# Two transformer blocks on one core: norm scales folded into the transposing product, the norm between the blocks rewritten, three up pieces in the last group

## The chip, the core and the metric

The kernel runs on one core of one Trainium2 chip. The metric is the device time of one execution in microseconds (us), lower is better. The engines are named as the profile names them: PE is TensorE (matmuls; PEld is its weight load), DVE is VectorE, ACT is ScalarE, POOL is GpSimd, SP is SyncE, whose queue issues the weight loads.

## The reference

Two blocks follow one another on 256 tokens of width 1024, in float32. The first has gated linear attention and sparse attention, a cross attention to 256 memory rows and a product-key expert layer ("peer"); the second has a gated recurrence (hgrn), a long convolution (hyena) and another peer layer. Each part starts with an RMS norm over the row. Two of these norms meet between the blocks: the first block's final norm, and the second block's first norm of its result.

```python
def rms_norm(x, g):
    y = x * lax.rsqrt(jnp.mean(x * x, axis=-1, keepdims=True) + EPS)
    return y * g

def first_block(x, mem, ...):
    hn = rms_norm(h, norm_mix)
    h = h + concat([gla_mixer(...), nsa_mixer(...)]) @ w_out
    h = h + cross_attn(rms_norm(h, norm_xattn), rms_norm(mem, norm_mem), ...)
    h = h + peer_ffn(rms_norm(h, norm_ffn), ...)     # 16384 experts, gelu(x @ down.T) * gate @ up
    return rms_norm(h, norm_final)

def second_block(x, ...):
    h = x + hybrid_mixer(rmsnorm(x, norm_mix_g), ...)
    h = h + peer_ffn_2(rmsnorm(h, norm_ffn_g), ...)
    return rmsnorm(h, norm_final_g)
```

The peer layers choose 16 experts per head for each token. The kernel computes them densely: all 16384 down products, a gate that is zero where an expert was not chosen, and all 16384 up products.

## The kernel before

**Products in three terms.** Each float32 operand is split into a high part (rounded to the fp32r type) and a low part (the rest), and `mm3` (L344 to L346) adds three products: high by high, low by high, high by low. A weight tile of 128x1024 is read by `load` (L250) on SP's queue into `wf`, of which there are four buffers, so a load starts when the tile four before it has been used up. `stream` makes the two parts: `wh` by an ACT cast (L318), `wl` by a DVE subtraction (L325, some of them on POOL), three buffers each. `dfth`, `dftl`, `idfth` and `idftl` (L491, L492) are the same two parts of the Fourier matrices that the second block needs; they are made while the first block ends. Behind most loads SP also issues a write of zeros of 512 KB (`gates<-zero`, L265), by which the second peer layer's gate table is cleared.

**A norm ahead of a product.** `norm_cols` turns 256 rows into columns for PE. `norm_rows` squares and sums each row in two halves (L391 on ACT, one on DVE), adds the halves (L410), forms mean plus epsilon (L381), raises it to the power -1/2 on POOL (L382), and scales the rows into a tile `xn`: three halves on DVE (L403), one on ACT (L404). This runs for the tokens' first half (t = 0) and second half (t = 1). `to_cols` then turns each 128x128 piece of `xn` on PE (L420: eight pieces for t = 0, eight for t = 1, into four PSUM banks of two pieces each), and `split` multiplies by the gain and makes the two parts `xch` (ACT, L430) and `xcl` (DVE, L433). There are five such sites: the start, the memory rows (about 95 to 110 us), the cross attention (213 to 229), and ahead of the two peer layers (`peer_in`, 316 to 328 and 1514 to 1523).

**Between the blocks.** `between` (L1416 to L1442, 1124 to 1141 us) does both norms at once. For each half of the tokens and each half of the columns it adds the peer sum from PSUM to the residual (L1425, `hres`), multiplies by the final gain (L1427, `hmid`), and takes the squares of both (`ssh` of `hres`, `ssy` of `hmid`). From the two sums follow two factors by small DVE operations (L1431 to L1434) and two POOL powers (L1437): one scales `hmid` to the second block's input, the other `hmid` to the first block's result (L1442, a whole row of 1024 each). `xn` is made by L1438 (DVE) and L1439 (ACT), and turned and split as above. The first tiles of the second block (`w2t`) are streamed behind it.

**The end of a peer layer.** `up` (L1082 to L1099) takes the 128 up tiles one by one: 12 matmuls of 128x512 for each, three on each of the four accumulating banks (two halves of the tokens by two halves of the columns). `ah` (ACT, L1078) and `al` (DVE, L1080) are the parts of the gated activations. The last two tiles are taken together, bank by bank, so that the first banks are complete earlier than the last. Behind the second peer layer `finish` (L1444 to L1461) adds, norms and writes the result.

**What sets the order.** Each engine works through its queue in order. A scheduler puts the instructions in an order by priorities; `after` adds an order between two instructions on one engine, and in `stream` and `norm_rows` it holds the first weight parts behind a norm (`self.ahead`).

## Time and profile before

| | us |
|---|---|
| timed, median of 3 runs | 2361.08 (2359.76 to 2364.35) |
| profiled execution, its own time | 2355.96 |
| span in the profile | 2354.2 |
| PE busy | 2307.6 |
| PE not busy | 46.6 |
| DVE, ACT, POOL busy | 1675.5, 1240.8, 471.6 |

The profiled execution is 5.12 us (0.2%) under the median of the timed runs. Busy times are taken over the whole span, so an engine that is nearly always busy hides the places where it waits; these places are found in the timeline, where each group of instructions has its start, its length and, in brackets, how long its engine was idle before it and what ended the wait. "PEclk" is the clock that TensorE was granted, as a share of 2.4 GHz: 0.50 is 1.2 GHz. A matmul's own length overlaps that of the next, so the distance between two starts is what one costs.

### The profile page before, as it was taken

To read this page: it belongs to the slowest core of one execution; us is meant where nothing else is said; L and a number is where in the kernel's file an instruction comes from. 1 tells how busy PE (TensorE), PEld (TensorE's weight loads), DVE (VectorE), ACT (ScalarE), POOL (GpSimd) and SP (SyncE) were. 2 spreads that over 40 slices of the span, in tenths; PEclk is the share of its full clock that TensorE was granted. 3 is DMA by queue.
4 is the path that set the end of the run, shared out by engine and by line. 5 is a ranking of instruction groups with operands and counts; after the bars stand their busy time and mean duration, and the time that the engine had idled before them with its cause. 6 is when DMAs were issued, how large, how long until landed. Compare 5 with 4: busy or idle time off the path is not lost.

```text
span 2354.2 us, 40890 instructions
## 1 busy us (share of the span) xinstructions
PE 2307.6 (98%) x15390; PEld 2100.5 (89%) x15390; DVE 1675.5 (71%) x3300; ACT 1240.8 (53%) x2368; POOL 471.6 (20%) x324
## 2 busy tenths in 40 slices
PE   8999999999999999999899999999999999999998
PEld 6976889999999888888899999899999999888886
DVE  6677559896677666666778886679886676666665
ACT  6555445456666444544654434445456665444444
POOL 0002000678760000000100000200787720000000
PEclk9999999999999999999999999999999999999999
DMA  7433565676555666666754444556675555666664
GB/s 236 137 119 98 161 224 170 175 185 161 149 148 155 221 201 201 197 201 194 249 173 130 150 153 144 181 175 183 164 187 152 149 148 194 198 203 199 203 202 134
DMA packets 149767, 412.26 MB, mean 175 GB/s; under 512 B 35980, under 2 KB 51521, under 8 KB 148417
## 3 DMA queue, kind: packets, MB, share of 16 engines
q1 hardware_dynamic: 129088, 409.57, 55.1%
q0 software_dynamic: 20480, 0.08, 2.4%
q8 instruction: 121, 1.98, 0.3%
q14 instruction: 78, 0.63, 0.1%
HBM read 394.83 MB, written 14.22 MB: 174 GB/s over the span
## 4 chain that ended last, share of the span: by engine, by line
PE 90%; DVE 7%; issue 1%; ACT 1%; POOL 1%; DMA 0%; POOLq 0%; SPq 0%; ACTq 0%
PE lin L346 16%; PE lin L344 16%; PE lin L345 16%; PE bank L346 11%; PE bank L344 11%; PE bank L345 10%; PE bank L1044 4%; DVE wl L325 2%; PE bank L1314 1%; PE bank L420 1%; PE bank L713 0%; ACT wh L318 0%; PE bank L832 0%; DVE cand L964 0%; POOL rstd L382 0%
## 5 line engine op out<-in xcount | busy, mean ns | idle before, releaser
L325 DVE TENSOR_TENSOR wl<-wf,wh 128x1024 fp32r<-128x1024 f32 (+1 forms) x698 | 853.3, 1224 | 301.7 <-ACT wh L318 296.8
L318 ACT CAST wh<-wf 128x1024 fp32r<-128x1024 f32 x704 | 734.8, 1045 | 610.2 <-PE lin L345 445.3
L344 PE MATMUL lin<-xch,wh 128*128 128x256 f32 x2912 | 836.6, 288 | 1.1 <-ACT wh L318 1.1
L346 PE MATMUL lin<-xch,wl 128*128 128x256 f32 x2912 | 827.5, 284 | 2.7 <-DVE wl L325 1.9
L345 PE MATMUL lin<-xcl,wh 128*128 128x256 f32 x2912 | 826.0, 284 | 0.0
L346 PEld LDWEIGHTS lin<-xch,wl 128*128 128x128 f32 x2912 | 559.3, 192 | 4.8 <-DVE wl L325 3.2
L344 PEld LDWEIGHTS lin<-xch,wh 128*128 128x128 f32 x2912 | 560.5, 193 | 3.0 <-ACT wh L318 1.4
L345 PEld LDWEIGHTS lin<-xcl,wh 128*128 128x128 f32 x2912 | 559.9, 192 | 0.0
L287 POOL DMA_INDIRECT gates<-gn,at x256 | 411.6, 1608 | 329.1 <-DVE gn L999 114.4
L346 PE MATMUL bank<-wh,al 128*128 128x512 f32 x1024 | 404.2, 395 | 0.0
L344 PE MATMUL bank<-wh,ah 128*128 128x512 f32 x1024 | 404.2, 395 | 0.0
L345 PE MATMUL bank<-wl,ah 128*128 128x512 f32 x1024 | 404.2, 395 | 0.0
L345 PEld LDWEIGHTS bank<-wl,ah 128*128 128x128 f32 x1024 | 192.6, 188 | 45.9
L344 PEld LDWEIGHTS bank<-wh,ah 128*128 128x128 f32 x1024 | 192.6, 188 | 45.8
L346 PEld LDWEIGHTS bank<-wh,al 128*128 128x128 f32 x1024 | 192.6, 188 | 45.8
L382 POOL TENSOR_TENSOR rstd<-rstd,mhalf 128x1 f32<-128x1 f32 (+1 forms) x18 | 13.3, 741 | 802.4 <-DVE rstd L381 737.2
L1078 ACT CAST ah<-Hb 128x256 fp32r<-128x256 f32 x128 | 52.0, 407 | 182.5 <-PE bank L345 182.5
L1078 ACT CAST ah<-Ha 128x256 fp32r<-128x256 f32 x128 | 52.0, 407 | 177.4 <-PE bank L345 175.4
L1043 ACT ACTIVATE c<-e,g 128x128 f32<-128x128 bf16 x384 | 132.7, 402 | 0.0
L1050 DVE TENSOR_TENSOR Ha<-bank,Ha 128x256 f32<-128x256 f32 x96 | 40.8, 425 | 104.6 <-PE bank L1044 102.4
L1080 DVE TENSOR_TENSOR al<-Hb,ah 128x256 fp32r<-128x256 f32 x128 | 54.5, 425 | 69.8 <-ACT ah L1078 68.5
L1080 DVE TENSOR_TENSOR al<-Ha,ah 128x256 fp32r<-128x256 f32 x128 | 54.4, 425 | 65.8 <-ACT ah L1078 65.5
(421 smaller groups left out, 2647.3 us busy)
## 6 DMA issues: line engine op xcount, KB each, us to landing
wf<-in_p_dn_dram SPq DMA_DIRECT2D x256, 512.0 KB
wf<-in_p_up_dram SPq DMA_DIRECT2D x256, 512.0 KB
wf<-in_w2t_dram SPq DMA_DIRECT2D x64, 512.0 KB
wf<-in_p_wq_dram SPq DMA_DIRECT2D x24, 512.0 KB
wf<-in_w_out_dram SPq DMA_DIRECT2D x16, 512.0 KB
gates<-zero SPq DMA_DIRECT2D x16, 512.0 KB
gt<-gates SPq DMA_DIRECT2D x32, 256.0 KB
wf<-in_w2k_dram SPq DMA_DIRECT2D x16, 512.0 KB
```

Source lines behind the costliest of these rows:

```text
L287: d = self.nc.gpsimd.indirect_dma_start(G[:, :], bass.IndirectOffsetOnAxis(ap=at[:, q:q + 1], axis=0), g[0:NS, q:q + 1], None, compute_op= ...
L318: hi = self.hi = nc.scalar.copy(wh[:, :n], wf[:, :n]).ins
L325: lo = eng.tensor_tensor(out=wl[:, :n], in0=wf[:, :n], in1=wh[:, :n].bitcast(F32), op=ALU.subtract).ins
L344: mm(out, a[0], b[0], start=start, stop=False)
L345: mm(out, a[0], b[1], start=False, stop=False)
L346: self.mm = mm(out, a[1], b[0], start=False, stop=stop).ins
L420: nc.tensor.transpose(b[:, t * P:(t + 1) * P], src[:, t, (c - c0) * P:(c - c0 + 1) * P], self.ident)
L1043: nc.scalar.mul(c[:, x], e[:, t4 + x], gf[:, t0 + t4 + x:t0 + t4 + x + 1])
L1044: nc.tensor.matmul(b[:, :, x], a[:, t4 + x], c[:, x], start=True, stop=True)
L1050: nc.vector.tensor_tensor(out=hv[:, :n], in0=bv[:, :n], in1=hv[:, :n], op=ALU.mult)
L1078: self.nc.scalar.copy(ah, hj)
L1080: self.nc.vector.tensor_tensor(out=al, in0=hj, in1=ah.bitcast(F32), op=ALU.subtract)
```

## The change

1. **Norm scales.** `norm_rows` makes no `xn`. It makes, for each half of the tokens, a diagonal matrix: the identity with each row multiplied by that token's factor (`scales`, a DVE operation of 128x128). `to_cols` multiplies the unscaled rows by it in an ordinary float32 matmul, which turns and scales at once, where it had turned `xn` with the identity. This is so at all five sites and between the blocks; the other users of `to_cols` keep the plain turn. The pools of `xn` go.
2. **Between the blocks.** The two powers of a half become one POOL operation of 128x2. The scaling of `hmid` by the first factor comes behind the second diagonal matrix. The first four weight tiles of the next block are held: their `wh` stands behind the last square on ACT, their `wl` behind the last diagonal matrix on DVE.
3. **Up.** In both peer layers the last three tiles are taken together, with three buffers for the activations' parts where there were two.

```diff
-            self.nc.scalar.activation(scr, x, AF.Square, accum_out=ss)
-    def norm_rows(self, h, xn, urgent):
+            self.sq = self.nc.scalar.activation(scr, x, AF.Square, accum_out=ss).ins
+    def scales(self, r):
+        d = self.small.tile([P, P], F32, name="diag", tag="diag", bufs=2)
+        self.dg = self.nc.vector.tensor_scalar(d, self.ident, r, None, op0=ALU.mult).ins
+        return d
+    def norm_rows(self, h, urgent):
...
-        r = [self.rstd_of(ss[t]) for t in range(2)]
-        for t, k in ((0, 0), (0, 1), (1, 0)):
-            nc.vector.tensor_scalar(xv[:, t, k], hv[:, t, k], r[t], None, op0=ALU.mult)
-        nc.scalar.mul(xv[:, 1, 1], hv[:, 1, 1], r[1])
+        d = [self.scales(self.rstd_of(ss[t])) for t in range(2)]
...
-                nc.tensor.transpose(b[:, t * P:(t + 1) * P], src[:, t, (c - c0) * P:(c - c0 + 1) * P], self.ident)
+                rows = src[:, t, (c - c0) * P:(c - c0 + 1) * P]
+                if diag:
+                    nc.tensor.matmul(b[:, t * P:(t + 1) * P], rows, diag[t], start=True, stop=True)
+                else:
+                    nc.tensor.transpose(b[:, t * P:(t + 1) * P], rows, self.ident)
...
+            if self.held[0] > 0:
+                self.held[0] -= 1
+                self.after(hi, self.held[1])
+                self.after(lo, self.held[2])
...
-        for js in [(j,) for j in range(P - 2)] + [(P - 2, P - 1)]:
+        for js in [(j,) for j in range(P - 3)] + [range(P - 3, P)]:
...
-            pa = e(tc.tile_pool(name="pact", bufs=2))
+            pa = e(tc.tile_pool(name="pact", bufs=3))
...
-            for q in (sy, sh):
-                nc.gpsimd.tensor_tensor(q[:, 0:1], q[:, 0:1], self.mhalf, op=ALU.pow)
-            nc.vector.tensor_scalar(xv[:, t, 0], yv[:, t, 0], sy[:, 0:1], None, op0=ALU.mult)
-            nc.scalar.mul(xv[:, t, 1], yv[:, t, 1], sy[:, 0:1])
-            r1.append(sh)
-        for t in range(2):
-            nc.vector.tensor_scalar(y[:, t], y[:, t], r1[t][:, 0:1], None, op0=ALU.mult)
+            nc.gpsimd.tensor_tensor(r, r, self.mhalf[:, 0:1].to_broadcast([P, 2]), op=ALU.pow)
+            d2.append(self.scales(r[:, 1:2]))
+            r1.append(r)
+        self.held = [4, self.sq, self.dg]
+        return r1, d2
...
+            r, d = self.between(h, acc, g, self.h)
+            x = self.cols("xc")
+            self.to_cols(self.h, x, range(8), lambda c: self.gains[:, 32 + c:33 + c], diag=d)
+            for t in range(2):
+                self.after(self.nc.vector.tensor_scalar(self.h[:, t], self.h[:, t], r[t][:, 0:1], None, op0=ALU.mult).ins, self.dg)
```

The change renumbers the lines of the kernel after it, so the same statement has another line there. The order of the queues moves at three places that matter here.

DVE between the blocks, before, from the second half's first small operation (L1431) to the second weight tile; `wl` is the weights' low part, `xcl` that of the columns:

```order
L1431 TENSOR_TENSOR ssh<-ssh 128x1
L492 TENSOR_TENSOR idftl<-wf,idfth 128x256
L1432 TENSOR_SCALAR ssh<-ssh 128x1
L1442 TENSOR_SCALAR hmid<-hmid,ssh 128x1024
L1431 TENSOR_TENSOR ssy<-ssy 128x1
L1433 TENSOR_SCALAR ssh<-ssh 128x1
L492 TENSOR_TENSOR idftl<-wf,idfth 128x256
L1434 SCALAR_TENSOR_TENSOR ssy<-ssy,ssh 128x1
L492 TENSOR_TENSOR idftl<-wf,idfth 128x256
L1438 TENSOR_SCALAR xn<-hmid,ssy 128x512
L1442 TENSOR_SCALAR hmid<-hmid,ssh 128x1024
```

These are followed by one `idftl`, six `xcl` and the first `wl`. The same place after:

```order
L1441 TENSOR_TENSOR ssh<-ssh 128x1
L502 TENSOR_TENSOR idftl<-wf,idfth 128x256
L1442 TENSOR_SCALAR ssr<-ssh 128x1
L1441 TENSOR_TENSOR ssy<-ssy 128x1
L1443 TENSOR_SCALAR ssh<-ssr 128x1
L1444 SCALAR_TENSOR_TENSOR ssr<-ssy,ssh 128x1
L400 TENSOR_SCALAR diag<-ident,ssr 128x128
L1498 TENSOR_SCALAR hmid<-hmid,ssr 128x1024
L325 TENSOR_TENSOR wl<-wf,wh 128x1024
L444 SCALAR_TENSOR_TENSOR xcl<-bank,gains,xch 128x256 x5
L325 TENSOR_TENSOR wl<-wf,wh 128x1024
```

The long scaling of `hmid` moved from ahead of the second `xn` to behind the second diagonal matrix, and the first `wl` from behind six `xcl` to ahead of them. Further up, not shown, both `dftl` moved ahead of the second addition.

ACT at the same place, before, from the last three squares to the second weight tile:

```order
L391 ACTIVATE lin,ssy<-hmid 128x512
L391 ACTIVATE lin,ssh<-hres 128x512
L1439 ACTIVATE xn<-hmid,ssy 128x512
L391 ACTIVATE lin,ssy<-hmid 128x512
L1439 ACTIVATE xn<-hmid,ssy 128x512
L491 CAST idfth<-wf 128x256
L430 ACTIVATE xch<-bank,gains 128x256 x6
L318 CAST wh<-wf 128x1024
L430 ACTIVATE xch<-bank,gains 128x256 x2
L318 CAST wh<-wf 128x1024
```

The same place after:

```order
L395 ACTIVATE lin,ssy<-hmid 128x512
L501 CAST idfth<-wf 128x256
L395 ACTIVATE lin,ssh<-hres 128x512
L395 ACTIVATE lin,ssy<-hmid 128x512
L318 CAST wh<-wf 128x1024
L441 ACTIVATE xch<-bank,gains 128x256 x5
L318 CAST wh<-wf 128x1024
L441 ACTIVATE xch<-bank,gains 128x256 x3
```

The two scalings are gone, the last square follows the one ahead of it, and the first `wh` moved from behind six `xch` to ahead of all.

PE in the last group of the first peer layer, after, with buffer numbers; banks 9028 and 9029 are the first half's two, and the weights' parts 11938/11940, 11949/11951 and 11960/11962 are those of the last three tiles:

```order
L348 MATMUL bank_9028<-wh_11949,ah_11954 128x512
L349 MATMUL bank_9028<-wl_11951,ah_11954 128x512
L350 MATMUL bank_9028<-wh_11949,al_11956 128x512
L348 MATMUL bank_9028<-wh_11960,ah_11965 128x512
L348 MATMUL bank_9029<-wh_11938,ah_11943 128x512
L349 MATMUL bank_9029<-wl_11940,ah_11943 128x512
L350 MATMUL bank_9029<-wh_11938,al_11945 128x512
L348 MATMUL bank_9029<-wh_11949,ah_11954 128x512
L349 MATMUL bank_9028<-wl_11962,ah_11965 128x512
L350 MATMUL bank_9028<-wh_11960,al_11967 128x512
```

In the same place before, the group had two tiles:

```order
L344 MATMUL bank_9039<-wh_11972,ah_11977 128x512
L345 MATMUL bank_9039<-wl_11974,ah_11977 128x512
L346 MATMUL bank_9039<-wh_11972,al_11979 128x512
L344 MATMUL bank_9039<-wh_11983,ah_11988 128x512
L345 MATMUL bank_9039<-wl_11985,ah_11988 128x512
L346 MATMUL bank_9039<-wh_11983,al_11990 128x512
L344 MATMUL bank_9040<-wh_11972,ah_11977 128x512
```

The first bank's last two products moved behind four of the second bank, so the last tile's `wl` is first used by the group's twelfth matmul of 36, and the first bank is complete with the thirteenth; before, that was the sixth of 24.

## Rows read from the trace of the kernel before

**Rows 1.** The page, part 1: busy us, share of the span, instructions of each engine.

```profile
PE 2307.6 (98%) x15390; PEld 2100.5 (89%) x15390; DVE 1675.5 (71%) x3300; ACT 1240.8 (53%) x2368; POOL 471.6 (20%) x324
```

**Rows 2.** Stretches: length, busy PE, PEld, DVE, ACT, POOL (count), PEclk, DMA, GB/s.

```profile
105.00:108.00 3.00, 3.00 (x19) 3.00 (x18) 1.36 (x5) 1.18 (x3) 0.00 (x0) 0.63 0.22 35
196.00:246.00 50.00, 46.48 (x307) 38.04 (x306) 31.61 (x60) 25.55 (x54) 12.61 (x12) 1.00 0.39 123
316.00:328.00 12.00, 9.07 (x46) 7.90 (x45) 6.65 (x17) 6.51 (x14) 4.36 (x4) 0.72 0.78 274
1122.00:1133.00 11.00, 7.09 (x32) 5.42 (x31) 9.12 (x20) 8.14 (x22) 1.86 (x2) 1.00 0.77 252
1133.00:1143.00 10.00, 6.61 (x26) 4.71 (x26) 7.83 (x20) 6.88 (x14) 1.19 (x2) 0.51 0.93 330
1514.00:1523.00 9.00, 6.06 (x33) 4.99 (x32) 5.43 (x15) 5.13 (x13) 2.91 (x3) 0.81 0.64 215
```

**Rows 3.** Timeline of TensorE between the blocks: start, length, work, [idle before, releaser].

```profile
1128.27 0.39 PE L345 MATMUL bank<-wl,ah 128*128 128x512 f32 x1
1128.50 0.40 PE L346 MATMUL bank<-wh,al 128*128 128x512 f32 x1
1132.81 1.65 PE L420 MATMUL bank<-ident,xn 128*128 128x128 f32 x8 [3.91 <-DVE xn L1438]
1135.86 1.12 PE L420 MATMUL bank<-ident,xn 128*128 128x128 f32 x4 [1.40 <-DVE xn L1438]
...
1139.97 0.58 PE L344 MATMUL lin<-xch,wh 128*128 128x256 f32 x1 [1.11 <-ACT wh L318]
...
1141.23 0.58 PE L346 MATMUL lin<-xch,wl 128*128 128x256 f32 x1 [0.25 <-DVE wl L325]
```

**Rows 4.** Timeline of VectorE, same place and columns.

```profile
1121.68 1.23 DVE L325 TENSOR_TENSOR wl<-wf,wh 128x1024 fp32r<-128x1024 f32 x1 [0.52 <-ACT wh L318]
...
1124.73 0.69 DVE L1425 TENSOR_TENSOR hres<-bank,hres 128x512 f32<-128x512 f32 x1 [0.77 <-PE bank L346]
...
1132.26 0.48 DVE L1438 TENSOR_SCALAR xn<-hmid,ssy 128x512 f32<-128x512 f32 x1 [0.44 <-POOL ssy L1437]
...
1133.13 0.74 DVE L1442 TENSOR_SCALAR hmid<-hmid,ssh 128x1024 f32<-128x1024 f32 x1
```

**Rows 5.** Timelines of GpSimd, ScalarE and SyncE's DMA queue, same place.

```profile
1131.30 0.93 POOL L1437 TENSOR_TENSOR ssy<-ssy,mhalf 128x1 f32<-128x1 f32 x1
...
1128.89 0.40 ACT L491 CAST idfth<-wf 128x256 fp32r<-128x256 f32 x1 [0.62 <-DMA wf<-in_idft_dram]
...
1132.89 0.58 ACT L391 ACTIVATE lin<-hmid 128x512 f32<-128x512 f32 x1
...
1138.88 1.04 ACT L318 CAST wh<-wf 128x1024 fp32r<-128x1024 f32 x1
...
1141.94 1.04 ACT L318 CAST wh<-wf 128x1024 fp32r<-128x1024 f32 x1 [0.44 <-DMA wf<-in_w2t_dram]
...
1134.40 0.48 SPq L250 DMA_DIRECT2D wf<-in_w2t_dram  x1
```

**Rows 6.** Timelines of TensorE, then VectorE, at the norm ahead of the first peer.

```profile
319.69 1.06 PE L420 MATMUL bank<-ident,xn 128*128 128x128 f32 x8 [2.28 <-DVE xn L403]
321.40 1.12 PE L420 MATMUL bank<-ident,xn 128*128 128x128 f32 x4 [0.65 <-DVE xn L403]
...
319.05 0.88 DVE L403 TENSOR_SCALAR xn<-hin,rstd 128x512 f32<-128x512 f32 x2 [0.66 <-POOL rstd L382]
```

**Rows 7.** Lines L420 and L1294: min/median/max ns, first and last start.

```profile
L420 PE MATMUL bank<-ident,hot x16: 270/272/329, 1448.8 to 1471.3; 128*128 128x128 f32 x16
...
L1294 PE MATMUL bank<-Q,ks x32: 275/275/347, 1278.5 to 1354.7; 128*128 128x128 f32 x32
```

**Rows 8.** Timeline of VectorE in the last norm.

```profile
2345.43 0.69 DVE L1451 TENSOR_TENSOR hres<-bank,hres 128x512 f32<-128x512 f32 x1
2346.04 0.14 DVE L381 TENSOR_SCALAR rstd<-ss 128x1 f32<-128x1 f32 x1
```

More of the change, by code (lines that the diff above doesn't have):

```diff
@@ L226, in __init__ @@
         self.ahead = 3
-        self.los = []
+        self.los, self.held = [], [0]
         self.blank, self.heads = iter(()), {}
@@ L296, in gates @@
     def gates(self, G, j, pool):
-        g = pool.tile([P, 8, NS], F32, name="gt")
+        g = pool.tile([P, 8, NS], F32, name="gt", bufs=2)
         d = self.nc.sync.dma_start(g.rearrange("p j t -> p (j t)"), G[1][:, j * NS:j * NS + 8 * NS]).ins
@@ L390, in square @@
         else:
-            self.nc.scalar.activation(scr, x, AF.Square, accum_out=ss)
-    def norm_rows(self, h, xn, urgent):
+            self.sq = self.nc.scalar.activation(scr, x, AF.Square, accum_out=ss).ins
[4 more added lines that the diff above has]
+    def norm_rows(self, h, urgent):
         nc = self.nc
-        hv, xv = (y.rearrange("p t (a d) -> p t a d", a=2) for y in (h, xn))
+        hv = h.rearrange("p t (a d) -> p t a d", a=2)
         ss = [self.small.tile([P, 2], F32, name="ss", tag="ss") for _ in range(2)]
@@ L411, in rstd_of, with to_cols @@
         return self.rstd(ss[:, 0:1], D, 1)
-    def to_cols(self, src, dst, chunks, gain=None, c0=0):
+    def to_cols(self, src, dst, chunks, gain=None, c0=0, diag=None):
         nc = self.nc
@@ L438, in cols, with norm_cols @@
         return (p.tile([P, 8, T], F32R, name=tag + "h", tag=tag + "h"), p.tile([P, 8, T], F32R, name=tag + "l", tag=tag + "l"))
-    def norm_cols(self, h, gi, dst, pool, xn=None, urgent=False):
-        xn = pool.tile([P, 2, D], F32, name="xn", tag="xn", bufs=1) if xn is None else xn
-        self.norm_rows(h, xn, urgent)
+    def norm_cols(self, h, gi, dst, urgent=False):
+        diag = self.norm_rows(h, urgent)
         dst = dst or self.cols("xc")
-        self.to_cols(xn, dst, range(8), lambda c: self.gains[:, gi * 8 + c:gi * 8 + c + 1])
+        self.to_cols(h, dst, range(8), lambda c: self.gains[:, gi * 8 + c:gi * 8 + c + 1], diag=diag)
         return dst
@@ L570, in block1_mix @@
             p, pn = pool("b1"), pool("nsa")
-            with tc.tile_pool(name="b1n", bufs=1) as px:
-                x = self.norm_cols(self.h, 0, None, px)
+            x = self.norm_cols(self.h, 0, None)
             h2 = self.filter_net(pf)
@@ L1414, in hyena, with between @@
             yield
-    def between(self, h, acc, g, y, xn):
+    def between(self, h, acc, g, y):
         nc = self.nc
-        hv, yv, xv = (u.rearrange("p t (a d) -> p t a d", a=2) for u in (h, y, xn))
-        r1 = []
+        hv, yv = (u.rearrange("p t (a d) -> p t a d", a=2) for u in (h, y))
+        r1, d2 = [], []
         for t in range(2):
-            sh, sy = [self.small.tile([P, 2], F32, name="ss" + n, tag="ss" + n) for n in "hy"]
+            sh, sy, r = [self.small.tile([P, 2], F32, name="ss" + n, tag="ss" + n) for n in "hyr"]
             for k in range(2):
@@ L1431, in between @@
                 nc.vector.tensor_tensor(out=q[:, 0:1], in0=q[:, 0:1], in1=q[:, 1:2], op=ALU.add)
-            nc.vector.tensor_scalar(sh[:, 0:1], sh[:, 0:1], 1.0 / D, EPS, op0=ALU.mult, op1=ALU.add)
-            nc.vector.tensor_scalar(sh[:, 1:2], sh[:, 0:1], EPS, None, op0=ALU.mult)
-            nc.vector.scalar_tensor_tensor(out=sy[:, 0:1], in0=sy[:, 0:1], scalar=1.0 / D, in1=sh[:, 1:2],
+            nc.vector.tensor_scalar(r[:, 0:1], sh[:, 0:1], 1.0 / D, EPS, op0=ALU.mult, op1=ALU.add)
+            nc.vector.tensor_scalar(sh[:, 1:2], r[:, 0:1], EPS, None, op0=ALU.mult)
+            nc.vector.scalar_tensor_tensor(out=r[:, 1:2], in0=sy[:, 0:1], scalar=1.0 / D, in1=sh[:, 1:2],
                                            op0=ALU.mult, op1=ALU.add)
-            for q in (sy, sh):
-                nc.gpsimd.tensor_tensor(q[:, 0:1], q[:, 0:1], self.mhalf, op=ALU.pow)
-            nc.vector.tensor_scalar(xv[:, t, 0], yv[:, t, 0], sy[:, 0:1], None, op0=ALU.mult)
-            nc.scalar.mul(xv[:, t, 1], yv[:, t, 1], sy[:, 0:1])
-            r1.append(sh)
-        for t in range(2):
-            nc.vector.tensor_scalar(y[:, t], y[:, t], r1[t][:, 0:1], None, op0=ALU.mult)
+            nc.gpsimd.tensor_tensor(r, r, self.mhalf[:, 0:1].to_broadcast([P, 2]), op=ALU.pow)
[3 more added lines that the diff above has]
+        return r1, d2
     def finish(self, h, acc, g):
@@ L1462, in peer_in @@
         self.nc.sync.dma_start(self.hsave, self.h)
-        with self.tc.tile_pool(name="pxn", bufs=1) as xp:
-            return self.norm_cols(self.h, gi, None, xp, urgent=True)
+        return self.norm_cols(self.h, gi, None, urgent=True)
     def build(self):
@@ L1486, in build @@
             self.h = ph.tile([P, 2, D], F32, name="hmid")
-            with tc.tile_pool(name="b2n", bufs=1) as pn:
-                xn = pn.tile([P, 2, D], F32, name="xn")
-                self.between(h, acc, g, self.h, xn)
-                x = self.cols("xc")
-                self.to_cols(xn, x, range(8), lambda c: self.gains[:, 32 + c:33 + c])
+            r, d = self.between(h, acc, g, self.h)
[3 more added lines that the diff above has]
+                self.after(self.nc.vector.tensor_scalar(self.h[:, t], self.h[:, t], r[t][:, 0:1], None, op0=ALU.mult).ins, self.dg)
             G = self.grid("gates2")
```

6 lines of the change are left out of this document (3 added, 3 removed).

## The prediction

> **What bounds the kernel now.** I read the page's busy times first. TensorE (PE) is busy for 2307.6 of 2354.2 us, every other engine far less [rows 1]. So work taken off VectorE, ScalarE or GpSimd is worth something only where PE stands still for it, and all such places together hold 46.6 us. The change touches those at the norms, so I read next the stretches around them [rows 2], where two things count: PE's idle time and its granted clock. At the norm ahead of the first peer layer PE is busy for 9.07 of 12 us at a mean clock of 0.72; at the one ahead of the second, 6.06 of 9 at 0.81; between the blocks 7.09 of 11 at full clock and then 6.61 of 10 at 0.51, which is nearly all at 1.2 GHz. In the timeline of PE between the blocks [rows 3] the reader is to see a chain: the last up product starts at 1128.50, PE waits 3.91 us for the first `xn`, 1.40 us for the second, then 1.11 us for the first `wh` and 0.25 us for the first `wl`; only from then on do products follow each other without waits. What stands behind these waits is in the rows of the other engines [rows 4, 5].
>
> **Norm scales, ahead of the two peer layers.** Removed for each site: three DVE scalings and one ACT scaling of 128x512. Added: two DVE operations of 128x128. A DVE scaling takes 0.48 us for 512 columns and 0.74 for 1024 [rows 4], 0.26 for 512 more, so 128 columns are estimated at 0.48 - 0.75 x 0.26 = 0.28 us. PE's 16 products stay 16: a turn with the identity takes 270 ns at full clock, an ordinary float32 product of the same size 275 [rows 7]. I put this at nothing. On the path at 316 us [rows 6]: the first turn started when the first of two scalings was done; with 0.28 for 0.48 it comes 0.2 us earlier. The second half's sum stood behind both scalings (0.88 us from 319.05); now it stands behind 0.28, so 0.5 to 0.6 earlier, and its own last step is again 0.2 shorter. The second turn, and with it the first product, comes about 0.75 us earlier. The site at 1514 us has the same instructions: two times 0.75 is **-1.5 us**. Bounds are -0.4 (only the shorter last steps count, and the second turn waits for something else) and -1.7 (the first PE wait of 2.28 shrinks too).
>
> At the start the first weight's arrival ends the wait after the norm, at the memory rows PE has other products, so both count nothing, within 0.3 us each. At the cross attention the scheduler has set the work around the norm in another order: the filter work of the hyena part now lies behind the norm, among the products of the memory keys. PE idles for 3.5 of 50 us there [rows 2]. The work is the same and only its place differs; I take nothing, with bounds of -1.5 and +1.5, less than half of that idle time either way.
>
> **Last three up tiles together.** The group has 36 products at 0.23 us [rows 3], 8.4 us, so it starts at about 1120.33, and its first bank is complete with the 13th, at about 1123.6. The first addition, which waited for that bank, started at 1124.73 [rows 4] and can come 1.1 us earlier. The price is that the third tile's `wl` is needed by the twelfth product, at 1120.33 + 11 x 0.233 = 1122.90. Before, that `wl` ran from 1121.68 for 1.23 us, to 1122.91 [rows 4], so PE waits for about 0.05 us, with no reserve. Bounds: 0, and the 0.52 us that this subtraction had itself waited for its cast, at each of two sites. I take **+0.1 us**.
>
> **Between the blocks, first half.** Before, the second power started at 1131.30 and took 0.93 [rows 5], the scaling followed at 1132.26 with 0.48, and the turns at 1132.81. One power goes: its neighbour took as long, so -0.93. That a power of two columns costs as much as one of one column isn't shown; the ends are a gain of nothing and of 0.93, and I take the latter, one start in place of two. The diagonal in place of the scaling is -0.2. Then the power starts earlier: ScalarE had stood 0.62 us for the Fourier matrix's load at 1128.89 [rows 5], whose buffer came free with a subtraction that now stands ahead of the second addition, and the additions start earlier by up to 1.1. I take -0.9 of this. Together -2.1: the turns start near 1130.7.
>
> **Second half.** The last bank's addition can't move, since the last product ends at 1128.9. But the last square, which ran at 1132.89 behind a scaling [rows 5], now follows its neighbour, at about 1131.6. The following small operations, one power (0.66, what VectorE waited for one at 319.05 [rows 6]) and the diagonal give a second diagonal matrix at about 1133.5 and turns right behind it, where they started at 1135.86 [rows 3]: -2.3. I keep 1133 to 1134.5.
>
> **From there to the full pace.** On VectorE the scaling of `hmid` (0.74) and the first `wl` (1.23) now stand between the second diagonal and the first `xcl`. They hold it until 1133.5 + 1.97 = 1135.5; PE covers most of this with the second half's turns, eight, 1.65 us by the first half's [rows 3]. Before, the first `wh` ran at 1138.88 [rows 5], behind six `xch`, and the first product started at 1139.97; now `wh` stands ahead of them and is done before the first `xch`, so the first product starts near 1134.6. After it PE goes at VectorE's pace, five `xcl` and a second `wl`. It had been without waits 1.5 us after its first product (1139.97 to 1141.5); I allow 2.7 here, since the first `xcl` is now what comes late, which gives 1137.3. That is **-4.2 us**; by the ends of the second diagonal, and by what the DMA brings, -2.0 to -5.5.
>
> **Last norm.** In `finish` the first half's mean stood behind the addition of the last bank (0.69 from 2345.43 [rows 8]). It now stands ahead of it and its power lies beside the last products, but the scaling and one multiplication now hold the last addition back by about 1 us of the 1.35 won. **-0.3 us**, bounds -0.5 and +0.3.
>
> **Sum.** -1.5 + 0.1 - 4.2 - 0.3 = -5.9 us on the profiled execution of 2355.96, which gives 2350.1. That execution is 5.1 us under the median of the timed runs, 2361.08, from which the same difference gives 2355.2. A measurement here tells about 0.2%, 4.7 us, from no change, so the forecast lies just outside.
>
> **Rivals.**
>
> *The clock stays up.* PE runs at half clock for (1 - 0.72) x 2 x 12 = 6.7 us at the first peer's norm, 3.4 at the second's, 9.8 between the blocks [rows 2]. If ordinary products, with shorter waits, kept it at 2.4 GHz, the two norms would give back half of the busy part, about 2.5 and 1.2 us, and the place between the blocks some 1.5, since there VectorE sets half of the pace: 5.2 us more, 2350. For it speaks that from 105 to 108 us, with turns and narrow products, PE was busy 3.00 of 3.00 us and the mean clock was still 0.63 [rows 2]. Against it, the waits of 1.7 to 2.2 us stay.
> The Trainium skill, in "TensorE: Matmul & The Clock Gate", Part 4 (PE-mode transpose), says that a product in transpose mode does not count as a busy PE for the clock gate. By that rule this rival would hold and give 2350; the row of 105 to 108 us agrees with it but holds other products as well, so it can't tell.
>
> *The weights don't come.* Between 1133 and 1143 us the DMA engines are 0.93 busy [rows 2]; the second `w2t` load was issued at 1134.40, and the cast that needed it waited until 1141.94 [rows 5]. Writes of zeros stand between the loads. The new order frees the buffers earlier, but the share was 0.77 in the 11 us before, so 2.5 us of transfer could be drawn ahead. If no more than 1.5 are, the 4.2 shrink to about 1.5 to 2, and the time is 2357.5 to 2359: within 0.2%.
>
> *Slower: filter work exposed at the cross attention.* GpSimd works for 12.61 us between 196 and 246 us [rows 2], mostly on the filters. It now starts behind the norm. If the products that need it come up before it is done, PE stands for it, and in the worst case for all of it: 2355.2 + 12.6 = 2367.8. It decides the sign from 10.6 us on, since 5.9 have to be eaten up first and 4.7 are the bound. Against it speaks that the stretch's products of memory keys and queries are long and don't need it.
>
> *The change doesn't shorten the diagonal path*: if two columns' power takes 1.87 and the diagonal as long as a scaling, between the blocks gives about 2.5, the norms 1.0: 2357.4, and so in the company of the second rival.
>
> **How the numbers follow.** My forecast, 2355.2, has 0.55 (own range 2352 to 2359), the clock 0.14, the weights and the diagonal path together 0.23, the exposed filter work 0.08. Faster by over 0.2% means under 2356.4: most of the forecast's chance (0.47) and all of the clock's, 0.61. Slower by over 0.2% is over 2365.8: the filter work and a little for a stall in both up groups, 0.09. The rest, 0.30, is within. The range, 2349.5 to 2361.5, takes in the clock's time and the weights', and leaves out the slower rival and the far end below.
>
> **What the profile after would show.** The first turn between the blocks should start 2 us after the last up product, the second near 5, the first product near 6, and PE should be without waits 8.5 us after it, where it was 13. At the peer norms the waits should be about 2.1 and 0.1 to 0.2 us. The twelfth product of the up group should show a wait under 0.5 us. Wrong would be: a `w2t` cast with a DMA as its releaser and PE behind it; a granted clock well over 0.8 at the first peer's norm (the clock's rival); PE idle for much more than 3.5 us around the cross attention.

## The result, and the profile after

The changed kernel takes 2342.48 us (median of 6 runs, 2341.13 to 2345.95) against 2360.40 before (6 runs, 2356.77 to 2364.35): the ratio is 0.9927, with a 95% interval from 0.9914 to 0.9939. That is 17.9 us faster, three times the 5.9 forecast, and under the range. The profiled execution's span is 2339.4 us against 2354.2, 14.8 us less, and the search for the difference goes by that.

The page of after, part 1 (busy us, share of the span, instructions), beside [rows 1]:

```profile
PE 2298.2 (98%) x15486; PEld 2113.1 (90%) x15486; DVE 1669.9 (71%) x3295; ACT 1237.8 (53%) x2361; POOL 466.0 (20%) x322
```

PE is busy for 9.4 us less, though it has 96 instructions more: each of the 96 turns by a diagonal counts as two. Less waiting, all that the forecast spoke of, can't do that. So I took the start of the same product in both traces at the ends of each stage, and noted by how much it had moved:

| stretch (us of before) | change, us | forecast |
|---|---|---|
| start to the end of the cross attention (0 to 317) | +7.8 | 0 (-1.5 to +1.5) |
| norm ahead of the first peer layer (317 to 343) | -1.7 | -0.75 |
| first down loop | -0.1 | 0 |
| **first up loop (770 to 1128)** | **-9.9** | +0.05 |
| between the blocks (1128 to 1213) | -3.3 | -4.2 |
| norm ahead of the second peer layer (1514 to 1550) | +0.8 | -0.75 |
| second mixer and second down loop | +0.3 | 0 |
| **second up loop (1988 to 2345)** | **-8.4** | +0.05 |
| last norm | -0.3 | -0.3 |
| sum | -14.8 | -5.9 |

More than the whole gain lies in the two up loops, in which the change was to touch only the last group; the norms gave what was left, and the first block took 7.8 us away. In the middle of the first up loop, the timeline of TensorE (start, length, work), first before and then after, from one `wh` by `ah` product to the one twelve products on:

```profile
899.83 0.40 PE L344 MATMUL bank<-wh,ah 128*128 128x512 f32 x1
...
902.63 0.40 PE L344 MATMUL bank<-wh,ah 128*128 128x512 f32 x1
```

```profile
900.09 0.39 PE L348 MATMUL bank<-wh,ah 128*128 128x512 f32 x1
...
902.81 0.39 PE L348 MATMUL bank<-wh,ah 128*128 128x512 f32 x1
```

Twelve products take 2.80 us before and 2.72 after: 0.2333 against 0.2267 each. It is so for each of the 1536 products of the loop up to the last group, with PE without a wait there in both, and 1536 x 0.0067 is 10.2 us. In the second loop before they took 0.2324, after again 0.2267: 8.8 us.

Between the blocks, what the forecast spoke of came nearly as told. Timeline of TensorE between the blocks, after; the last up product starts at 1124.55:

```profile
1126.65 2.02 PE L429 MATMUL bank<-diag,hmid 128*128 128x128 f32 x16 [1.72 <-issue]
1129.59 1.16 PE L429 MATMUL bank<-diag,hmid 128*128 128x128 f32 x8 [0.91 <-DVE diag L400]
1131.22 0.39 PE L348 MATMUL lin<-xch,wh 128*128 128x256 f32 x1 [0.47 <-ACT xch L441]
1132.50 0.79 PE L429 MATMUL bank<-diag,hmid 128*128 128x128 f32 x2 [0.90 <-DVE xcl L444]
```

The turns start 2.1 us after the last up product (4.3 before, [rows 3]), those of the second half 5.0 after it (7.4), the first product 6.7 (11.5), and the last wait ends 8.0 after it (12.7).

The power of two columns, on GpSimd, and the norm ahead of the first peer layer, on TensorE:

```profile
1125.52 0.71 POOL L1446 TENSOR_TENSOR ssr<-ssr,mhalf 128x2 f32<-128x2 f32 x1 [429.97 <-DVE ssr L1444]
```

```profile
327.20 2.94 PE L429 MATMUL bank<-diag,hin 128*128 128x128 f32 x24 [1.99 <-DVE diag L400]
```

Each of the first half's two powers had taken about 0.93 [rows 5]; one of two columns takes 0.71. At the norm, twelve turns now run without the wait of 0.65 us that had parted them [rows 6], but as 24 instructions: an ordinary float32 product leaves two in the trace, a turn in transpose mode one. They start 0.116 us apart here, and in [rows 6] eight turns took 1.06 us, 0.113 apart, so a turn by the diagonal costs PE twice as much.

In the first block the clock moved. Stretches with length, busy time of PE, PEld, DVE, ACT, POOL (count), granted clock, DMA share and GB/s; first before, then after:

```profile
94.00:112.00 18.00, 17.49 (x136) 16.77 (x134) 13.45 (x30) 13.20 (x29) 1.11 (x2) 0.91 0.56 182
112.00:130.00 18.00, 18.00 (x130) 16.84 (x130) 10.77 (x31) 7.07 (x19) 2.03 (x2) 0.91 0.17 50
```

```profile
94.00:112.00 18.00, 18.00 (x155) 17.60 (x154) 13.21 (x29) 13.15 (x28) 1.59 (x3) 1.00 0.62 210
112.00:130.00 18.00, 18.00 (x91) 15.65 (x90) 7.93 (x18) 3.15 (x8) 1.51 (x2) 0.62 0.01 2
```

While the memory rows are turned (94 to 112) the clock now stays up; but in the 18 us behind that it stands at a mean of 0.62, that is at 1.2 GHz for three quarters of the time, with PE busy throughout.

### The profile page after: what moved, and what is told of

Read it like the earlier page. It is cut to its first block, busy times and chain, and to the rows that moved or that the text cites. A ratio compares the mean times of both kernels' runs of the same rounds, so it can differ in the third digit from the quotient of the medians.

```text
span 2339.4 us, 41023 instructions
## 1 busy us (share of the span) xinstructions
PE 2298.2 (98%) x15486; PEld 2113.1 (90%) x15486; DVE 1669.9 (71%) x3295; ACT 1237.8 (53%) x2361; POOL 466.0 (20%) x322
## 4 chain that ended last, share of the span: by engine, by line
PE 89%; DVE 7%; issue 1%; DMA 1%; ACT 1%; POOL 0%; SPq 0%; POOLq 0%; ACTq 0%
PE lin L350 16%; PE lin L348 16%; PE lin L349 16%; PE bank L348 10%; PE bank L350 10%; PE bank L349 10%; PE bank L1053 4%; DVE wl L325 2%; PE bank L1323 1%; PE bank L429 1%; ACT wh L318 0%; PE bank L841 0%; PE bank L722 0%; DVE cand L973 0%; PE bank L925 0%
## 5 line engine op out<-in xcount | busy, mean ns | idle before, releaser
L349 PE MATMUL bank<-wl,ah 128*128 128x512 f32 x1024 | 398.6, 389 | 0.0
L350 PE MATMUL bank<-wh,al 128*128 128x512 f32 x1024 | 398.4, 389 | 0.0
L348 PE MATMUL bank<-wh,ah 128*128 128x512 f32 x1024 | 398.3, 389 | 0.0
L386 POOL TENSOR_TENSOR rstd<-rstd,mhalf 128x1 f32<-128x1 f32 (+1 forms) x18 | 12.7, 707 | 794.9 <-DVE rstd L385 729.7
L1053 PE MATMUL bank<-c,a 128*128 128x128 f32 x768 | 101.4, 275 | 0.0
```

The costliest lines, as they stand in the source:

```text
L348: mm(out, a[0], b[0], start=start, stop=False)
L349: mm(out, a[0], b[1], start=False, stop=False)
L350: self.mm = mm(out, a[1], b[0], start=False, stop=stop).ins
L1053: nc.tensor.matmul(b[:, :, x], a[:, t4 + x], c[:, x], start=True, stop=True)
```

## Experiments

### Where the operands stand in memory

What differs in the up loop? Three activation buffers in place of two, casts that run a tile ahead, and one thing that no line of the change says. The pool of small tiles grew by two diagonal matrices (2 x 512 bytes per partition) and four tiles of the two factors (4 x 32), so every tile allocated behind it stands 1152 bytes further. In the built program `ah` stood at 84480 and 85504 and `al` at 90624 and 91648, multiples of 512; now all stand 128 bytes past one. The weights `wh` and `wl` stand 128 bytes past a multiple of 512 in both. The first experiment gives the kernel before these 128 bytes and nothing else, the second takes them from the changed kernel; the order on every engine stays that of the kernel each was made from.

```diff
 # pad128: the kernel before;  unpad: the changed kernel, with 96 for 32
         self.small = e(tc.tile_pool(name="small", bufs=4))
+        self.small.tile([P, 32], F32, name="pad", tag="pad", bufs=1)
```

> The kernel before with one unused tile of 128 bytes per partition in the pool of small tiles, so that every tile behind it, among them the up products' stationary parts ah and al, stands 128 bytes further, as in the changed kernel. The instructions and their order on every engine are the kernel before's. Theory of place (where the stationary operand lies in the memory sets what one product costs): the up products go from 0.2333 and 0.2324 us to 0.2267 in both peers, 1536 products each, so the time falls by 10.2 + 8.8 us and a little for four shorter stretches, to about 2341. Rival (the third activation buffer and the casts that run one tile ahead make the products faster): no difference to the kernel before, 2360.

Measured: 2338.46 us against 2357.05 for the kernel before beside it, ratio 0.9921 (0.9905 to 0.9938), 18.6 us. Its timeline of TensorE, twelve products apart as above:

```profile
899.92 0.39 PE L345 MATMUL bank<-wh,ah 128*128 128x512 f32 x1
...
902.64 0.39 PE L345 MATMUL bank<-wh,ah 128*128 128x512 f32 x1
```

2.72 us, as in the changed kernel. So 128 unused bytes do alone as much as the whole change did (its 17.9 us lie within the interval), and the buffers play no part in the up products' price.

> The changed kernel with one unused tile of 384 bytes in the same pool, which puts ah and al back to multiples of 512 bytes, where they stood before. Order unchanged. Theory of place: the up products go back to 0.2333 us and the time rises by about 19 us, to about 2361, so the change itself without the place gains nothing. Rival (third buffer, casts one tile ahead): 2342, the same as the changed kernel.

Measured: 2361.60 us against 2357.05, ratio 1.0014 (1.0004 to 1.0024), and products of 0.2333 us:

```profile
899.64 0.40 PE L349 MATMUL bank<-wh,ah 128*128 128x512 f32 x1
...
902.44 0.40 PE L349 MATMUL bank<-wh,ah 128*128 128x512 f32 x1
```

Without its place the change is no gain; if anything it is slower. This fits the table above: some 4 us won from the first peer's norm on, the clock's part among them, and 7 to 8 lost in the first block.

The third asks whose start counts. Tiles are larger by 512 bytes and a slice of them is used, whose start moves on by 32 bytes every eight tiles.

```diff
 # scan: the kernel before
-        ah = pool.tile([P, T], F32R, name="ah", tag=tag)
+        ah = pool.tile([P, T + pad], F32R, name="ah", tag=tag)[:, o:o + T]
-            wh = self.pw.tile([P, 1024], F32R, name="wh", tag="wh", bufs=3)
+            wh = self.pw.tile([P, 1152], F32R, name="wh", tag="wh", bufs=3)[:, wo:wo + 1024]
 # al and wl alike; first peer: o = wo(down) = 8 * (j // 8); second peer, up: o = 32, wo = 8 * (j // 8)
```

> The kernel before, same order, with larger tiles of which a slice is used: in the first peer's up products the stationary parts start 0, 32, 64, ... 480 bytes into a 512-byte cell, eight tiles each; in its down products the stationary weights' parts start 128, 160, ... bytes in; in the second peer's up products the stationary parts start at 128 and the moving weights' parts at 128, 160, ... Theory of place by the stationary operand's own start: in the first peer 0.2267 us at 128 and 0.2333 at 0, 32 and 160, where the kernel before and the changed one show these; in the second peer 0.2267 throughout. Theory of place by the distance of the two operands: in the second peer 0.2267 only where the moving part is at 128 too. Rival (buffers): no difference between the places.

Two of its stretches in the first peer's up loop, with 72 products between the rows of each: stationary parts at 128, then at 160.

```profile
860.33 0.39 PE L346 MATMUL bank<-wh,ah 128*128 128x512 f32 x1
...
876.65 0.39 PE L346 MATMUL bank<-wh,ah 128*128 128x512 f32 x1
...
882.17 0.40 PE L346 MATMUL bank<-wh,ah 128*128 128x512 f32 x1
...
898.97 0.40 PE L346 MATMUL bank<-wh,ah 128*128 128x512 f32 x1
```

16.32 / 72 is 0.2267, 16.80 / 72 is 0.2333. All stretches, put by the distance of the stationary from the moving operand's start, modulo 256 bytes:

| distance | 0 | 32 | 64 | 96 | 128 | 160 | 192 | 224 |
|---|---|---|---|---|---|---|---|---|
| first peer (stationary moved), us | 0.2267 | 0.2333 | 0.2333 | 0.2342 | 0.2325, 0.2332 | 0.2333 | 0.2289 | 0.2333 |
| second peer (moving moved), us | 0.2267 | 0.2332 | 0.2332 | 0.2344 | 0.2333 | 0.2333 | 0.2289 | 0.2333 |

The two rows agree, so the distance counts and not where either operand stands; the rule by the stationary operand's own start, which had also fitted both kernels, is out. The same run moved the stationary weights of the first peer's down products (256 columns) against the fixed `xch`. There equal starts, which this kernel has, are among the worst: 0.1199 us at distance 0, as much at 160, 0.117 to 0.120 at the others, and 0.1143 in eight tiles at 64. The eight later tiles at the same distance modulo 256 (320, a start of 448) took 0.1178.

### The first block's loss

The next kernel takes the changed one and does the first block's three norms as before; the one after it only that of the memory rows.

```diff
 # oldnorm_b1 (start, memory rows, cross attention);  oldnorm_mem (memory rows only)
-                    self.norm_cols(hm, 2, mc)
+                    self.norm_cols(hm, 2, mc, xn=hm)     # scale by DVE and ACT into xn, then turn xn
```

> The changed kernel with the first block's three norms (start, memory rows, cross attention) done as before, with scaled rows and plain turns; the two peer norms, the place between the blocks and the up groups stay changed. In the changed kernel's trace the work up to 317 us ends 7.8 us later than before, with the clock at 0.50 from about 112 to 128 us. Theory (the diagonal products there moved the order and with it the stretch at half clock): 7 to 8 us faster than the changed kernel, about 2335. Rival (the loss comes from elsewhere, or the old order falls to half clock as well): within 2 us of 2342.

> The changed kernel with only the norm of the memory rows done as before; the start and the cross attention keep the diagonal products. Theory (the loss of the first block comes from the memory rows' norm, after which the clock stands at 0.50 from 112 to 128 us): as fast as with all three norms done as before, 2335. Rival (it comes from the cross attention, where the order moved most): 2342, as the changed kernel.

Measured: 2335.11 us (0.9909, 0.9889 to 0.9929) and 2334.62 (0.9907, 0.9891 to 0.9924). The changed kernel had 2342.48, so the loss of some 7 us is that of the memory rows' norm alone. With it as before, the stretch from 112 to 130 us is back at a clock of 0.91:

```profile
112.00:130.00 18.00, 18.00 (x129) 16.73 (x128) 11.04 (x30) 7.20 (x19) 1.26 (x2) 0.91 0.15 51
```

Two things changed there: the turns became ordinary products, and the scheduler set TensorE's products from 95 to 230 us in another order. The two kernels below part them.

```diff
 # mem_plain: oldnorm_mem, xn turned by an ordinary product with the identity (changed kernel's order)
+                    nc.tensor.matmul(b[:, t * P:(t + 1) * P], rows, self.ident, start=True, stop=True)
 # mem_forced: oldnorm_mem, turns as before, but its 627 products of the stretch tied into mem_plain's order
+        for x, y in zip(names, names[1:]):
+            self.after(self.rec[y], self.rec[x])
```

> The same kernel with the scaled memory rows turned by ordinary products with the identity. The scheduler then gives the changed kernel's order to within a few instructions. Both theories, of order and of the product's kind, expect 2340 to 2343 and one long stretch at 0.50 behind 112 us. If it is 2335, the loss lies in the scaling by the diagonal itself, which would be a third cause.

> The kernel with only the memory rows' norm done as before (2335 us: scaled rows, turned in transpose mode), but with TensorE's products from 95 to 230 us put, by hand, into the order that the changed kernel has there. Theory of order (the changed order, in which narrow products stand between the 256-column ones, keeps the clock at 0.50 for some 16 to 20 us after the memory norm): 2340 to 2343, as the changed kernel. Theory of the product's kind (ordinary products for the turns keep the clock up until 112 us and then it falls for long): 2335, with short stretches at 0.50.

Measured: 2342.83 us (2341.77 to 2344.11) for the ordinary product, the whole loss without a diagonal. For the order alone 2340.62, but spread over 2334.76, 2340.14, 2341.10 and 2343.34. The profiled execution was the fastest of these, and in it the clock did not fall there; below are the stretches of the ordinary product and of the order alone:

```profile
94.00:112.00 18.00, 17.87 (x154) 17.48 (x152) 14.16 (x31) 13.69 (x29) 1.10 (x2) 1.00 0.60 200
112.00:130.00 18.00, 18.00 (x87) 15.81 (x86) 7.70 (x18) 2.42 (x6) 2.03 (x2) 0.58 0.04 15
```

```profile
94.00:112.00 18.00, 16.59 (x124) 15.65 (x123) 12.96 (x28) 12.87 (x28) 1.10 (x2) 0.91 0.61 195
112.00:130.00 18.00, 18.00 (x142) 16.62 (x141) 11.79 (x29) 7.76 (x20) 2.03 (x2) 1.00 0.12 39
```

The four kernels of this study that turn the memory rows by ordinary products all show 1.00 from 100 to 112 us and 0.57 to 0.62 behind it. The ten that turn them in transpose mode show 0.72 to 0.86 in the first stretch (one of them 1.00) and 0.90 to 1.00 (one of them 0.72) in the second. So the fall is put off and then lasts longer. The order alone stays open: its four times overlap the four of oldnorm_mem, which has the old order and the old turns (2331.93 to 2339.23), and they go with the clock, whose mean over the span was 0.997 in the fastest and 0.993 to 0.994 in the other three. Those three were not traced.

Nor is the clock the whole loss. From 94 us to the end of the cross attention the changed kernel and mem64 (below, with the memory rows' norm as before) both stand at 0.50 for 20.5 us in their traces, the kernel before for 6.8. Against the kernel before, mem64 had lost 4.5 us by then and the changed kernel 8.0. Of the 3.5 between them, the second instruction of each of the 16 turns is an estimated 16 x 0.113 = 1.8 us, since PE has no wait there; the 64 bytes of mem64 and the order share the rest.

### The group of three

```diff
 # group2: the changed kernel
-        for js in [(j,) for j in range(P - 3)] + [range(P - 3, P)]:
+        for js in [(j,) for j in range(P - 2)] + [range(P - 2, P)]:
```

> The changed kernel with the last two up tiles together, as before, in place of three; three activation buffers and all places stay. In the changed kernel the last tile's low weight part comes 0.43 us late in each peer. Theory: those two waits go, the first bank is complete about 1.1 us later, and the turns between the blocks start later by up to that; the up products stay at 0.2267 us. Together within 1.5 us of the changed kernel.

Measured: one time of 2344.02 us, 1.5 over the changed kernel's median. In the changed kernel's trace two products of the last group come late: the seventh, which needs the third tile's `wh`, and the twelfth, which needs its `wl`. The first row below holds two products, which take 0.56 us where 0.45 is usual; the twelfth takes 0.33 where 0.23 is usual.

```profile
1117.72 0.73 PE L348 MATMUL bank<-wh,ah 128*128 128x512 f32 x2
1118.28 0.40 PE L349 MATMUL bank<-wl,ah 128*128 128x512 f32 x1
...
1118.98 0.49 PE L349 MATMUL bank<-wl,ah 128*128 128x512 f32 x1
1119.31 0.39 PE L350 MATMUL bank<-wh,al 128*128 128x512 f32 x1
```

That is about 0.2 us, not the 0.43 of the expectation, which took the first row for one product. With two tiles the up loops are 0.28 us shorter each, the whole price. But between the blocks group2 gains 2.0 us over the kernel before where the group of three gains 3.3. So the three tiles are worth about 0.7 us by these two traces, which one time can't show.

### Better places

If distance counts, the down products can be had for less: 64 bytes ahead of the weight buffers put the stationary `wh` and `wl` 64 past `xch`, while `ah` and `al` move along with them and keep distance 0 in the up loop.

```diff
 # place64: pad128;  best64: oldnorm_b1;  mem64: oldnorm_mem;  place320: pad128, with 80 for 16
         self.pw = e(tc.tile_pool(name="w", bufs=1))
+        self.pw.tile([P, 16], F32, name="wpad", tag="wpad", bufs=1)
```

> The kernel with the 128 unused bytes (order of the kernel before), and 64 more unused bytes ahead of the weight buffers. Now wh and wl start 64 bytes behind the columns xch, modulo 256, where they had the same start, and ah and al keep the weights' own start. In the scan, down products with the weights 64 bytes further took 0.1143 us where the others took 0.117 to 0.120. Theory (the distance of stationary to moving operand modulo 256 sets the cost, and 64 is the good one for 256 columns): the 8736 products of the columns take 0.114 to 0.117 in place of 0.1199, 25 to 50 us less than with the 128 bytes alone (2338), so 2290 to 2313, and the up products stay at 0.2267. Rival (the scan's eight tiles were fast for another reason, or the down products are held by VectorE and the loads): within 5 us of 2338.

Measured: 2312.22 us, ratio 0.9812 (0.9796 to 0.9829), 26 us under pad128: the kernel before with 192 unused bytes and no other change. A stretch of the first down loop, before and then here, has 170 and 176 matmuls in the same 20 us, with PE busy throughout:

```profile
420.00:440.00 20.00, 20.00 (x170) 19.75 (x169) 15.50 (x48) 8.99 (x14) 13.94 (x9) 1.00 0.72 198
```

```profile
420.00:440.00 20.00, 20.00 (x176) 19.75 (x175) 16.06 (x48) 9.44 (x15) 13.93 (x8) 1.00 0.74 206
```

The down products took 0.1155 us on average where no wait lay between them, 0.1199 before; the second peer's 3072 took 408.6 us from first to last in place of 418.7.

> As the kernel with 64 unused bytes ahead of the weight buffers (2312 us, down products 0.1155 us), but with 320 bytes, so that the weights stand 64 bytes behind the columns modulo 256, and 320 modulo 512. If only the distance modulo 256 counts for the 256-column products, as the scan shows for the 512-column ones: 2312 again and 0.1155. If it is modulo 512, as the scan's 0.1178 at 448 against 0.1143 at 192 says: about 0.1175, and some 15 us more, near 2327. The up products stay at 0.2267 either way.

Measured: 2317.35 us (2314.03 to 2318.38), down products 0.1153. So 64 and 320 cost the same per product, and only the distance modulo 256 counts here too; why the scan's eight tiles at 448 took 0.1178 isn't shown. The 5 us more aren't in these products. They go with the clock: its mean over the span was 0.987 to 0.989 in these four runs and 0.990 to 0.992 in three of place64's, whose fourth, at 0.987, took 2317.62 us.

> The changed kernel with the first block's three norms done as before (2335 us) and the same 64 unused bytes ahead of the weight buffers. Theory of distance: as much faster than 2335 as the 64 bytes bring to the other kernel, 2287 to 2310. Rival: within 5 us of 2335.

> The changed kernel with only the memory rows' norm done as before (2335 us), and 64 unused bytes ahead of the weight buffers. With all three norms of the first block as before these bytes brought 25 us. Expected the same here: 2308 to 2312. Rival (the 64 bytes shift the stretches at half clock in the first block again): up to 2316.

Measured: 2310.20 us (0.9798, 0.9782 to 0.9815) and 2306.90 us (0.9787, 0.9754 to 0.9819; 2302.68 to 2315.32). Both beat the two kernels of this case. The second has the diagonal products everywhere but at the memory rows, and 64 bytes. Neither is clear of place64 (2312.22 us, 0.9796 to 0.9829), which is the kernel before with unused bytes alone.

## Why the prediction was wrong

- **The step that failed** is the first one: that only PE's waits can change, and work which the change does not name keeps its price. "The group has 36 products at 0.23 us" took the up products' cost from before, and the sum held terms for the norms, the place between the blocks and the last group alone. The change moved `ah` and `al` by 128 bytes, the distance to the weights went from 128 to 0, and 3072 products became 0.0057 to 0.0067 us cheaper: -19.0 us for which there was no term and no rival. Nothing in the change aimed at it; that the pool grew by just these bytes was luck.
- **The norm scales**, forecast at -1.5 us, gave nothing at equal clock. "PE's 16 products stay 16" and "I put this at nothing" compared the lengths of one instruction, 270 and 275 ns. [rows 7] lists 32 of them for L1294, which has 16 products in the kernel: an ordinary float32 product leaves two. The run of the scan shows it, because it has the norm as before and its clock stays at 1.00 there. TensorE at the first peer's norm in that run:

```profile
320.64 0.40 PE L348 MATMUL lin<-wh,xcatl 128*128 128x512 f32 x1
323.32 1.06 PE L422 MATMUL bank<-ident,xn 128*128 128x128 f32 x8 [2.28 <-DVE xn L405]
325.03 0.67 PE L422 MATMUL bank<-ident,xn 128*128 128x128 f32 x4 [0.65 <-DVE xn L405]
325.92 0.50 PE L346 MATMUL lin<-xch,wh 128*128 128x256 f32 x2 [0.22 <-ACT xch L432]
```

From the last product ahead of the norm to the first behind it is 5.28 us; in the changed kernel, also at 1.00, it is 5.22 (324.82 to 330.04):

```profile
324.82 0.40 PE L350 MATMUL lin<-wh,xcatl 128*128 128x512 f32 x1
327.20 2.94 PE L429 MATMUL bank<-diag,hin 128*128 128x128 f32 x24 [1.99 <-DVE diag L400]
330.04 0.50 PE L348 MATMUL lin<-xch,wh 128*128 128x256 f32 x2
```

The waits are 1.2 us shorter, about as told, and the doubled turns take that back. Over the first table's two stretches the scan moved by -1.8 and -0.4 us against the kernel before, and the changed kernels whose clock stays at 1.00 there by -1.7 and -0.4.
- **The first block.** "At the memory rows PE has other products, so both count nothing, within 0.3 us" fell: 7 us, measured by taking that norm back. PE did have other products, and just so the 16 turns' second instructions cost their full time, and what the products behind them cost depends on the clock. The bound there was for idle time, and none was added.
- **The clock's rival** was half right. At the first peer's norm, where [rows 2] had 0.72, the clock stayed at 1.00 in six of the nine kernels with the diagonal there, and in one of the five with the norm as before. So the -1.7 of the first table is the clock's: the scan has it without the change. At the second peer's norm the changed kernel's clock fell for 3.4 us, and the same stretch became 0.8 longer where five kernels with the same norm and no fall have -0.4. Between the blocks the time at 0.50 went from 10.2 us to 3.4, but it is worth little there: of the kernels with the group of three and the weights' old place, two with none of it gain 3.9 and 4.1 us, four with 3.4 us of it 3.3 to 3.9.
- **Between the blocks** -3.3 for -4.2, and each mark that the prediction had set was met within 0.7 us; the mechanism was right. The power of two columns took 0.71 us, as one start. The DMA rival came in small: its sign, a `w2t` cast with a DMA as its releaser and PE behind it, is there. On ScalarE the first cast waited 1.77 us for its load, and the first `xch` ran behind it, for which the first product waited 0.47 us:

```profile
1129.74 1.05 ACT L318 CAST wh<-wf 128x1024 fp32r<-128x1024 f32 x1 [1.77 <-DMA wf<-in_w2t_dram]
1130.69 1.56 ACT L441 ACTIVATE xch<-bank,gains 128x256 fp32r<-128x256 f32 x4
```

- **The group of three** cost 0.28 us at each end for 0.05. The last `wl` had "no reserve", the third tile's `wh` was not reckoned with, and the bound of 0.52 held.
- **The last norm** -0.3 as told. The mean stands ahead of the last addition now, unlike in [rows 8], and the scaling and a multiplication hold that addition back, as the timeline of VectorE shows:

```profile
2329.56 0.14 DVE L385 TENSOR_SCALAR rstd<-ss 128x1 f32<-128x1 f32 x1
2330.38 0.48 DVE L1463 TENSOR_SCALAR hres<-hres,rstd 128x512 f32<-128x512 f32 x1 [0.68 <-POOL rstd L386]
2330.78 0.68 DVE L1461 TENSOR_TENSOR hres<-hres,gfin 128x512 f32<-128x512 f32 x1
2331.39 0.68 DVE L1459 TENSOR_TENSOR hres<-bank,hres 128x512 f32<-128x512 f32 x1
```

- **Slower by exposed filter work** did not come: the cross attention's part of the first table is small beside the clock's (+6.9 us had been lost by 154 us, +8.3 by 256).

Granted clock in steps of 2 us from the last product ahead of the norm of the first peer, read from each kernel's stretches:

| kernel, norm there | 0 | 2 | 4 | 6 | 8 | 10 |
|---|---|---|---|---|---|---|
| before, pad128, place64, place320: as before | 1.00 | 0.63 to 0.95 | 0.50, 0.51 | 0.50 to 1.00 | 0.50 to 1.00 | 0.84 to 1.00 |
| scan: as before | 1.00 | 1.00 | 1.00 | 1.00 | 1.00 | 1.00 |
| after, unpad, group2, oldnorm_b1, mem_plain, mem_forced: diagonal | 1.00 | 1.00 | 1.00 | 1.00 | 1.00 | 1.00 |
| oldnorm_mem, best64, mem64: diagonal | 1.00 | 0.69 to 0.90 | 0.50 | 0.75 to 0.95 | 1.00 | 1.00 |

The sum of the terms that were forecast came to about -3.9 us, where -5.9 was told: -1.7 and +0.8 at the peer norms, -3.3 between the blocks, -0.3 at the last norm and +0.6 for the two groups of three. The place between the blocks and the last norm were right in kind; what the peer norms show is the clock. What the change was made for was the smallest of three effects.

## What to carry to other kernels

A change of pools moves every tile behind them, and here 128 bytes were worth more than all the work on waits: ahead of costing a change, compare the built program's tile starts with those of before, and test a suspicion by one unused tile. Where a loop of equal products fills most of the span, look at the distance between their starts first: a wait is worth its length once, a product's 7 ns were worth 19 us. Count a product's instructions in the trace, and not only the length of one. And a change at a place where the engine is never idle can still cost, by what it does to the clock of the work behind it.

## What the runs showed of the hardware

- A product of a 128x128 fp32r stationary and a 512-column fp32r moving operand starts every 0.2267 us where both operands' starts in a partition are equal modulo 256 bytes, every 0.2289 at a distance of 192, and every 0.2325 to 0.2344 at the other six multiples of 32 that were run. With 256 columns equal starts and a distance of 160 are the dearest, 0.1199, and 64 bytes gave 0.1153 to 0.1155 on average over whole loops. Why isn't shown: no wait of TensorE appears in the trace at either pace.
- An ordinary float32 product of 128x128 leaves two instructions, a turn in transpose mode one, and each starts 0.113 to 0.116 us after the one before at a clock of 1.00: 24 instructions of twelve products took 2.94 us, eight turns 1.06.
- TensorE's clock fell to 0.50 while PE was busy 18.00 of 18 us (112 to 130 us, mean 0.62). Behind ordinary turns it fell later and for longer, in four of four traces. What sets the length isn't shown: kernels with one and the same order there had 6.8 and 13.7 us at 0.50 between 94 and 170 us (before and pad128).
- The Trainium skill's rule in "TensorE: Matmul & The Clock Gate", Part 4 (PE-mode transpose), that a product in transpose mode does not count as a busy PE for the clock gate, agrees with the first half of this: with ordinary products the clock held at 1.00 until 112 us in four of four kernels, with the transpose mode in one of ten. At the first peer's norm it agrees in part: the clock fell there in four of five kernels with the transpose mode, but also in three of nine with ordinary products. The long stretch at half clock behind the memory rows is more than the rule says.
